# Attention keys split into a near band and far classes, and values projected by token: a change to a hybrid layer on one core

## The chip, the cores and the metric

The kernel runs on one core of a Trainium2 chip. The metric is the device time of one execution in microseconds (us), given as the median of several runs. Beside it stands one profiled execution, whose trace has the time of every instruction.

The engines are TensorE (PE in the profile, with its weight loads as PEld), VectorE (DVE), ScalarE (ACT), GpSimd (POOL) and SyncE (SP, which here only issues DMA transfers).

## The reference

One layer of a hybrid trunk, 1024 tokens of 1024 features, float32. The normalised input goes through one combined projection, whose columns feed two mixers: a gated delta rule (four heads of 128, chunked, with a short causal convolution) and a dilated attention (eight heads of 64). Their outputs are concatenated and projected, added to the input, and followed by a gated MLP. What the change touches is the attention:

```
DIL_PATTERNS = ((128, 1), (512, 4), (2048, 16))      # (window, dilation)
def dilated_attention(q, k, v):
    for window, dil in DIL_PATTERNS:                  # query t sees keys t, t-dil, ..., t-window
        num, den, m = band_attention(stride(qf), stride(kf), stride(vf), window // dil)
        ...
    out = sum(exp(m_i - m_all) * num_i) / sum(exp(m_i - m_all) * den_i)
```

Merging the branches by their denominators is the same as one softmax over all keys, in which a key that several branches see counts once per branch. A weight of 2 or 3 is a term log 2 or log 3 added to the score.

## The kernel before, in words

**Projections.** Every float32 matrix is split into a high and a low part in a faster format, and a product takes three matmuls (`mm3`: high x high, high x low, low x high). A projection tile is 128 columns of the combined weight: `raw_weight` loads 512 KB, `weight` splits them (high part on ScalarE, low part on VectorE), and 2 x 8 x 3 matmuls of 128 x 128 stationary weights and 512 moving tokens make 128 features x 1024 tokens. VectorE rescales the result by the token's norm. Raw tiles, high parts and low parts have two slots each, so a split waits until TensorE has left the tile two before. The loop is `dense` (line 477), its order is the list `DENSE` (line 42): one key tile of the delta rule, two attention tiles, four times queries and values of the delta rule, then the other ten attention tiles (of each of four head pairs: queries, keys, values), then four gate tiles (`z`). The attention's tiles are parked in DRAM (`apark`), with the tokens of each block of 128 sorted by class (token modulo 4), 32 tokens a class.

**Attention.** `attention` (line 865) works on four pairs of heads, eight blocks of 128 queries each, two blocks to a step. `att_load` reads queries, keys and values of a pair; `att_values` (line 844) transposes the values on TensorE to tokens x features (`vn`) and makes a second copy sorted by class (`vc`) with 16 small transfers. For each block, `scores` (line 884) makes the scores of the block itself and the one before it (the near part, 256 columns), and then the scores of each class of queries against the keys of the same class of blocks 0 to 3 (128 columns, for blocks 0 to 3) or 0 to 7 (256 columns, for blocks 4 to 7), near and even future ones among them; a mask with the multiplicities removes what is too much. The class products are 32 queries wide and several run side by side in the array. `softmax` (mask and minimum on VectorE, exponential on ScalarE, division on VectorE), `turn` (transposes, line 932), `values` (near part, line 946) and `merge_classes` (class part, line 955, once per four blocks) follow.

**Order.** A class `Weave` plays the streams (delta rule, attention, projections, output projection) against its own estimate of each engine's time and so fixes the order on TensorE by hand: every matmul gets a token. A stream with a lower number goes first when its operands are estimated ready; `dense` has the lowest rank and fills the gaps. So projection matmuls stand between the attention's steps. On the other engines and on SP's queue a scheduler orders the instructions at build time, and each engine then executes in that order; SP issues one DMA after the other, and one that waits for a semaphore holds those behind it. The recurrence (`chain`) starts when all its queries and values are projected and the blocks' inverses are merged (`forward_sub` on VectorE, `merge` on TensorE); `kprep` transposes the keys, makes their Gram products and stores blocks of them to DRAM; attention follows the chain; then the output projection and the MLP, which the change leaves as they are.

In the profile most instructions carry line 189 (`mm`), 193 (`tp`), 139 or 141 (the helper that records an engine's operation), so tiles are told apart by name: `sm` softmax, `pt` and `pb` its transposes (near and class part), `vn` and `vc` the values, `whi`, `wlo`, `xhi`, `xlo` the high and low parts of weights and input, `um` key blocks, `og` and `zz` the gate work, `olo` the output projection's split.

Of the kernel before, what the change touches and what calls it, by code (L numbers as in the profile page):

```python
# [7 lines left out]
F32 = mybir.dt.float32  # L8
# [7 lines left out]
P = 128  # L16
S = 1024
# [24 lines left out]
DENSE = ([("k", 3), ("a", 0, 0), ("a", 0, 1)] + [(c, h) for h in range(4) for c in "qv"] + [("a", 0, 2)]  # L42
         + [("a", p, i) for p in (1, 2, 3) for i in range(3)] + [("z", h) for h in range(4)])
# [101 lines left out]
def hybrid_layer(tc, I, out):  # L145
# [91 lines left out]
    apark = dp.tile([4, 3, P, S], F32, name="apark")  # L237
# [239 lines left out]
    def dense():  # L477
# [5 lines left out]
        raw = [raw_weight(I["wi"][0])]  # L483
        nxt = wk(None, raw.pop())
        raw.append(raw_weight(I["wi"][1]))
        for i, col in enumerate(DENSE):
            kind, h = col[:2]
            if kind == "z":
                yield from wv.until(("o", h))
            w = nxt  # L490
            if i + 1 < len(DENSE):
                nxt = wk(None, raw.pop())
            if i + 2 < len(DENSE):
                raw.append(raw_weight(I["wi"][i + 2]))
# [343 lines left out]
    def att_load(pi):  # L838
        qT, kT, vT = [A(nm, "uy") for nm in ("qT", "kT", "vT")]
        for i, t in ((2, vT), (0, qT), (1, kT)):  # L840
            sy.dma_start(t, apark[pi, i])
        return qT, kT, vT

    def att_values(vT):

        vn, vc = A("vn", "kt"), A("vc", "kt")
        for hh in range(2):
            pt = yield from next_bank("atr", vT, slack=ASLACK * (hh == 0))
            for c in range(4):
                i = 4 * hh + c  # L850
                tp(pt[:, c * P:(c + 1) * P], vT[:, i * P:(i + 1) * P])
            ac.activation(vn[:, half(hh)], pt, AF.Copy)
        queue = wv.free["sync"]
        for c in range(4):
            for n in range(4):
                sy.dma_start(vc[32 * n:32 * n + 32].rearrange("u (c b d) -> u c b d", c=4, b=2)[:, c],
                             vn[32 * c:32 * c + 32].rearrange("u (b n d) -> u n b d", b=2, n=4)[:, n])

        wv.ready[vc.tensor.name] = max(wv.pe, wv.ready[vn.tensor.name]) + 6.0
        wv.free["sync"] = max(wv.pe, queue) + 1.6  # L860
        return vn, vc
# [3 lines left out]
    def attention():  # L865
        for h in range(2):
            yield from wv.until(("c", h, NCH - 1))
        mks = [A("mk", "go") for _ in range(2)]
        sy.dma_start(mks[0], I["mk"][0])
        sy.dma_start(mks[1], I["mk"][1])  # L870
# [674 lines left out]
```

## Time and profile before

| what | us |
|---|---|
| median of three runs | 1243.48 |
| lowest and highest | 1238.09, 1244.25 |
| span of the profiled execution, first to last instruction | 1237.8 |
| TensorE busy in it | 1216.1 |
| VectorE busy | 960.1 |
| ScalarE busy | 576.7 |

The page of the profile gives no other time of the profiled execution beside its span, which is 0.3 us below the lowest run. In the trace the projections with the delta rule's preparation take roughly the first 200 us, the chain runs until about 290, the attention until about 500, and the output projection and the MLP take the rest.

### The profile page before, as it was taken

The page shows a single profiled execution, that of the slowest core. Times are in us where ns is not written, and L with a number is a line of the kernel's source. Part 1 is how long each engine was busy: PE and PEld are TensorE (multiplying, and loading weights), DVE is VectorE, ACT ScalarE, POOL GpSimd, SP SyncE. Part 2 cuts the span into 40 slices and gives each one's busy share as a digit, 9 for nine tenths or more (in the row PEclk, how much of TensorE's full clock was granted, in tenths as well). Part 3 has the DMA queues.
Part 4 walks back from the last instruction along what each step waited for, and adds up shares of the span by engine and source line. Part 5 has one row for each costly group of instructions (what it writes and reads, how often), then busy time and mean ns, then how long its engine had stood idle before and what let it go on. Part 6 is the DMA issues. An engine that isn't in the chain of part 4 may idle for free.

```text
span 1237.8 us, 18310 instructions
## 1 busy us (share of the span) xinstructions
PE 1216.1 (98%) x7040; PEld 1003.8 (81%) x7040; DVE 960.1 (78%) x1526; ACT 576.7 (47%) x1111; POOL 48.8 (4%) x34
## 2 busy tenths in 40 slices
PE   9999999999999999999999999999999999999996
PEld 7888887898777877788788888888888888788886
DVE  7686984573666758577889898898898989899875
ACT  7383344363443435455454454444444554344441
POOL 0211110022000000000000000000000000000000
PEclk9999999999999999999999999999999999999999
DMA  7423235245342311343321322312313298545623
GB/s 230 103 75 97 85 116 170 92 137 206 126 146 61 107 57 45 124 173 120 119 100 53 102 81 73 102 55 99 100 54 102 80 357 286 169 149 192 196 85 137
DMA packets 81975, 153.53 MB, mean 124 GB/s; under 512 B 21824, under 2 KB 32736, under 8 KB 81888
## 3 DMA queue, kind: packets, MB, share of 16 engines
q1 hardware_dynamic: 81888, 152.37, 37.7%
q8 instruction: 55, 0.90, 0.3%
q14 instruction: 32, 0.26, 0.1%
HBM read 114.31 MB, written 35.93 MB: 121 GB/s over the span
## 4 chain that ended last, share of the span: by engine, by line
PE 87%; DVE 7%; DMA 2%; issue 2%; ACT 1%; POOL 1%; POOLq 0%; DVEq 0%; ACTq 0%
PE ps L189 45%; PE pa L189 19%; PE dw L189 10%; PE pc L189 9%; PE ps L193 4%; DVE pr L139 2%; DMA wd<-in_wd 2%; DVE x1h L139 1%; DVE wd L139 1%; PE warm L189 1%; DMA wst<-in_wu 0%; DVE wlo L139 0%; DVE sm L141 0%; DVE t L139 0%; POOL rs L139 0%
## 5 line engine op out<-in xcount | busy, mean ns | idle before, releaser
L189 PE MATMUL dw<-pr 128*128 128x512 f32 (+1 forms) x984 | 212.5, 377 | 1.5 <-DVE x1h L139 1.3
L189 PEld LDWEIGHTS dw<-pr 128*128 128x128 f32 x984 | 176.2, 188 | 36.7 <-DVE x1h L139 3.3
L189 PE MATMUL ps<-xhi,whi 128*128 128x512 f32 x448 | 187.4, 418 | 0.0
L189 PE MATMUL ps<-xhi,wlo 128*128 128x512 f32 x448 | 176.2, 393 | 0.0
L189 PE MATMUL ps<-xlo,whi 128*128 128x512 f32 x448 | 175.4, 392 | 0.0
L189 PE MATMUL pa<-T,pair 128*128 128x512 f32 x528 | 127.1, 389 | 0.6 <-ACT u L139 0.6
L189 PEld LDWEIGHTS pa<-T,pair 128*128 128x128 f32 x528 | 98.9, 188 | 21.2 <-ACT u L139 0.7
L189 PEld LDWEIGHTS ps<-xhi,wlo 128*128 128x128 f32 x448 | 84.3, 188 | 18.8
L189 PEld LDWEIGHTS ps<-xhi,whi 128*128 128x128 f32 x448 | 84.7, 189 | 17.0 <-issue 3.3
L189 PEld LDWEIGHTS ps<-xlo,whi 128*128 128x128 f32 x448 | 84.9, 189 | 13.3
L139 ACT ACTIVATE u<-pa 128x512 f32<-128x512 f32 x44 | 26.3, 598 | 110.7 <-PE pa L189 110.7
L139 DVE SCALAR_TENSOR_TENSOR y<-xu,fcw,y 128x1023 f32<-128x1023 f32 (+1 forms) x44 | 56.3, 1280 | 25.7 <-ACT y L139 25.6
L139 ACT ACTIVATE whi<-wst 128x1024 fp32r<-128x1024 f32 (+2 forms) x38 | 38.5, 1013 | 58.2 <-PE ps L189 52.3
L189 PE MATMUL pc<-B,pair 128*128 128x512 f32 x264 | 63.4, 389 | 0.0
L189 PE MATMUL pa<-B,A 128*128 128x512 f32 x264 | 63.4, 389 | 0.0
L189 PE MATMUL pc<-T,S 128*128 128x512 f32 x264 | 63.4, 389 | 0.0
L189 PE MATMUL pa<-T,S 128*128 128x512 f32 x264 | 63.4, 389 | 0.0
L141 ACT ACTIVATE sm<-sm,mx 128x512 f32<-128x512 f32 (+2 forms) x64 | 41.2, 646 | 45.6 <-DVE mx L141 45.6
L139 DVE TENSOR_TENSOR wst<-wst 128x512 f32<-128x512 f32 x88 | 60.3, 686 | 0.8
L189 PE MATMUL ps<-B,pair 128*128 128x512 f32 x252 | 60.5, 389 | 0.0
L139 ACT ACTIVATE pr<-wd 128x1024 fp32r<-128x1024 f32 x33 | 34.9, 1058 | 49.6 <-DVE wd L139 28.3
L189 PEld LDWEIGHTS pc<-T,S 128*128 128x128 f32 x264 | 49.5, 188 | 10.3
(232 smaller groups left out, 2292.0 us busy)
## 6 DMA issues: line engine op xcount, KB each, us to landing
wst<-in_wu SPq DMA_DIRECT2D x44, 512.0 KB, 3.7
wd<-in_wd SPq DMA_DIRECT2D x44, 512.0 KB, 3.8
wst<-in_wi SPq DMA_DIRECT2D x25, 512.0 KB, 3.7
upark<-y SPq DMA_DIRECT2D x22, 512.0 KB, 3.7
apark<-aqkv SPq DMA_DIRECT2D x12, 512.0 KB, 2.8
r<-upark SPq DMA_DIRECT2D x11, 512.0 KB, 7.3
r<-upark SPq DMA_DIRECT2D x22, 256.0 KB, 7.2
wa<-in_wd SPq DMA_DIRECT2D x22, 256.0 KB, 2.7
```

What stands on the lines that cost most here:

```text
L139: return getattr(eng, op)(*a, **kw)
L141: return getattr(eng, op)(*a, **kw)
L189: tc.stamp_issue_order_token(nc.tensor.matmul(dst, lhs, rhs, start=start, stop=stop, **kw).ins, TOKEN)
L193: tc.stamp_issue_order_token(nc.tensor.transpose(dst, src, ident).ins, TOKEN)
```

## The change

It has three parts.

1. **Keys.** A block's class scores now cover only the blocks before its near part: blocks 0 and 1 have none, 2 and 3 have 64 columns, 4 and 5 have 128, 6 and 7 have 192. They stand ahead of the near scores in the row. The near mask now holds the multiplicities of all three branches, and one mask of 896 columns serves all blocks as a plain slice, where it was a strided view of two masks. `turn` transposes fewer 128-column pieces, and `merge_classes` uses 64 of the 128 class keys of the last group and only the blocks of queries that have it.
2. **Values.** The attention's value columns leave the list of tiles. They are projected to tokens x features straight away: the input's parts are stationary (128 tokens), the weights move (512 columns, all heads). Two groups of four token blocks, each with four weight tiles of 512 KB in which two of eight row blocks lie; the second group loads and splits the same weights again. ScalarE evicts with the token's norm as scale, and the result goes to DRAM (`vpark`). `att_values`, its transposes and its 16 transfers per pair go; `att_load` reads `vn` in four and `vc` in two transfers from `vpark`.
3. **Order.** In `DENSE` the two value groups stand right behind the first key tile, ahead of the delta rule's queries and values, where two attention tiles stood; eight attention tiles follow behind those.

```diff
-DENSE = ([("k", 3), ("a", 0, 0), ("a", 0, 1)] + [(c, h) for h in range(4) for c in "qv"] + [("a", 0, 2)]
-         + [("a", p, i) for p in (1, 2, 3) for i in range(3)] + [("z", h) for h in range(4)])
+DENSE = ([("k", 3), ("V", 0), ("V", 1)] + [(c, h) for h in range(4) for c in "qv"]
+         + [("a", p, i) for p in range(4) for i in range(2)] + [("z", h) for h in range(4)])
...
+        def values_by_token(g):
+            banks = [bank(t) for t in ("asc", "asc", "ch", "ch")]
+            for j in range(4):
+                w = [t.rearrange("p (k m) -> p k m", k=2) for t in take()]
+                for kk in range(2):
+                    k = 2 * j + kk
+                    for i, pt in enumerate(banks):
+                        c = 4 * g + i
+                        yield wv.need(pt, *w)
+                        mm3(pt, [t[:, c * P:(c + 1) * P] for t in xs[k]], [t[:, kk, :] for t in w], k == 0, k == KT - 1)
+            for i in range(0, 4, 2):
+                vx = A("vx", "ev", shape=(P, 2, 512))
+                for e in range(2):
+                    c = 4 * g + i + e
+                    ac.activation(vx[:, e, :], banks[i + e], AF.Copy, scale=rst[:, c:c + 1])
+                c = 4 * g + i
+                sy.dma_start(vpark[c * P:(c + 2) * P].rearrange("(e p) d -> p e d", e=2), vx)
+            wv.done.add(("V", g))
...
     def att_load(pi):
-        qT, kT, vT = [A(nm, "uy") for nm in ("qT", "kT", "vT")]
-        for i, t in ((2, vT), (0, qT), (1, kT)):
+        qT, kT = [A(nm, "uy") for nm in ("qT", "kT")]
+        for i, t in enumerate((qT, kT)):
             sy.dma_start(t, apark[pi, i])
...
+        for c in range(4):
+            sy.dma_start(v8(vn)[32 * c:32 * c + 32], by_class[c][:, :, cols])
...
+        for b in range(2):
+            sy.dma_start(vc.rearrange("p (b c d) -> p b c d", b=2, c=4)[:, b], rows[b][:, :, cols])
...
-                it["n1"] = (it["n"] + 1) * P - it["k0"]
-                it["wd"] = it["n1"] + P * it["nb"]
+                it["near"] = (n + 1) * P - it["k0"]
+                it["far"] = 64 * (n // 2)
+                it["wd"] = it["far"] + it["near"]
...
-                for c in range(4):
+                for c in range(4 if far else 0):
                     o = slice(32 * c, 32 * c + 32)
                     for e, er in enumerate(HALVES):
-                        mm(it["ps"][e][o, n1_:wd].rearrange("p (n u) -> p n u", u=32),
+                        mm(it["ps"][e][o, :far].rearrange("p (n u) -> p n u", u=32),
...
-                    for i in range(wd // P):
-                        tp(pp[:, i * P:(i + 1) * P], sm[:, e, i * P:(i + 1) * P])
-                    turned(it, e, pt, pp)
+                    for i in range(near // P):
+                        tp(pp[:, i * P:(i + 1) * P], sm[:, e, far + i * P:far + (i + 1) * P])
+                    for i in range(nf):
+                        tp(pp[:, near + i * P:near + (i + 1) * P], sm[:, e, i * P:(i + 1) * P])
...
+            parts = (((0, 128, 0), (1, 64, 2)) if hh else ((0, 64, 2),))
             for c in range(4):
-                for b in range(nb):
-                    for e in range(2):
+                for b, rows, u in parts:
+                    for e, er in enumerate(HALVES):
...
-                           vcv[:, c, b, er], g["pb"][e][:, :, b, 32 * c:32 * c + 32], 0.14,
+                           vcv[:rows, b, c, er], g["pb"][e][:rows, u:, b, 32 * c:32 * c + 32], 0.11 - 0.028 * u,
```

The number of matmuls that the projections take is the same before and after (25 tiles of 48, against 21 tiles of 48 and two groups of 96).

More of the change, by code (lines that the diff above doesn't have):

```diff
@@ L934, in turn @@
             for b, (it, tag) in enumerate(zip(pair, ("asc", "atr"))):
-                sm, wd, n1_ = it["sm"], it["wd"], it["n1"]
+                sm, near, far = it["sm"], it["near"], it["far"]
+                nf = -(-far // P)
                 it["pt"] = []
@@ L949, in values @@
                 u = it["u"]
-                for i in range(it["n1"] // P):
+                for i in range(it["near"] // P):
                     for e, er in enumerate(HALVES):
@@ L980, in attention, with advance @@
         pipe = []
-        def advance(pair, more=None):
+        def advance(pair):
             done = pipe.pop() if pipe else None
@@ L985, in advance @@
                 yield from turn(done)
-            if more is not None:
-                last["values"] = yield from more
             if pair is not None:
```

147 lines of the change are left out of this document (70 added, 77 removed).

## The prediction

> **What bounds the kernel now.** I read the busy shares first, then the chain that ended last, then windows by stage, because a share over the whole span hides where the slack is.
>
> ```profile
> PE 1216.1 (98%) x7040; PEld 1003.8 (81%) x7040; DVE 960.1 (78%) x1526; ACT 576.7 (47%) x1111; POOL 48.8 (4%) x34
> PE 87%; DVE 7%; DMA 2%; issue 2%; ACT 1%; POOL 1%; POOLq 0%; DVEq 0%; ACTq 0%
> 60.00:80.00 20.00, 20.00 (x101) 16.68 (x100) 18.16 (x25) 18.63 (x70) 1.64 (x1) 1.00 0.17 55
> 100.00:200.00 100.00, 100.00 (x572) 84.48 (x571) 80.63 (x162) 40.69 (x113) 15.14 (x9) 1.00 0.37 111
> 290.00:440.00 150.00, 150.00 (x1333) 118.70 (x1332) 93.95 (x244) 62.60 (x163) 4.48 (x2) 1.00 0.36 117
> 440.00:500.00 60.00, 55.26 (x506) 43.50 (x505) 43.80 (x101) 27.16 (x64) 0.00 (x0) 0.97 0.21 59
> ```
>
> The columns of a window are its length, then busy time of PE, PEld, DVE, ACT and POOL, the granted clock, DMA share and GB/s. TensorE is the bound and also the chain. In the attention stage (290 to 440) it is busy for 150.00 of 150.00 us, since projection products stand between the attention's steps as filler. So work taken from TensorE here comes off the end one for one, and work taken from VectorE, ScalarE or the queues counts only where TensorE waits: the last 60 us (4.74 us idle). From 60 to 80 us ScalarE has only 1.37 us to spare and VectorE 1.84; the change puts work just there.
>
> **The change on TensorE.** The counts are from the order of both built kernels' instructions; matmuls of plain f32 have two records each in the trace.
>
> ```profile
> L193 PE MATMUL ps<-ident,sm 128*128 128x128 f32 x216 | 29.3, 276 | 3.7 <-DVE sm L141 3.7
> L189 PE MATMUL ps<-pb,vc 128*64 128x128 f32 x192 | 12.0, 273 | 0.0
> L189 PEld LDWEIGHTS ps<-pb,vc 128*64 128x64 f32 x192 | 11.0, 137 | 0.0
> L189 PE MATMUL ps<-kT,qT 64*32 64x256 f32 x256 | 8.8, 382 | 0.0
> L189 PE MATMUL ps<-kT,qT 64*32 64x128 f32 x256 | 5.3, 275 | 0.0
> L189 PEld LDWEIGHTS ps<-kT,qT 64*32 64x32 f32 x512 | 7.1, 106 | 6.3 <-issue 5.3
> 62.07 1.04 PE L193 MATMUL ps<-ident,kT 128*128 128x128 f32 x8
> 62.86 0.47 PE L189 MATMUL ps<-xhi,whi 128*128 128x512 f32 x1
> 70.22 0.39 PE L189 MATMUL ps<-xhi,wlo 128*128 128x512 f32 x1
> 77.56 1.05 PE L189 MATMUL ps<-kT 128*128 128x128 f32 x8
> 78.37 0.48 PE L189 MATMUL ps<-xhi,whi 128*128 128x512 f32 x1
> ```
>
> Busy over count is the price here; the mean beside it holds the pipeline's latency.
>
> 1. Class scores. Now 256 records of 256 columns at 34.4 ns (8.8/256) and 256 of 128 at 20.7 ns (5.3/256): 14.1 us. After: none for blocks 0 and 1, and 128 records each of 64, 128 and 192 columns. On the straight line through both prices, 64 and 192 columns cost 13.9 and 27.5 ns; 13.9 is also what a weight load of this shape takes (7.1/512). That makes 128 x (13.9 + 20.7 + 27.5) = 7.9 us: **-6.2**. If 64 columns cost as much as 128, -5.3; if half of it, -6.7.
> 2. Transposes of the softmax: 216 to 184. Eight transposes take 0.79 us from start to start of what follows (62.07 to 62.86), 0.099 each: 32 fewer are **-3.2**; by the group's 0.136 (waits in it), -4.3.
> 3. Transposes of the values: 32 fewer of the same kind, **-3.2** (up to -4.3). Their eight evictions and 64 small transfers go too, at no gain: TensorE doesn't wait for them.
> 4. Class values. 192 records stay 192, but 128 of them have 64 columns instead of 128. By columns that would be 128 x 31 ns = 4.0 us. But a record takes 62.5 ns (12.0/192) and its weight load 57 ns (11.0/192), and the load has the same 64 columns of values as before: 128 x 5 ns, **-0.7**. The Trainium skill, "TensorE: Matmul & The Clock Gate", section "LDWEIGHTS (loading the stationary operand)", says that a load takes its columns over 1.2 in ns whatever its rows; an estimate by it is 53 ns, so at most -1.2, and the halved contraction (64 of 128 rows) buys nothing. The trace's 57 ns agrees, which is why I don't book the 4.0.
> 5. Values by token: 192 matmuls of 512 columns replace 192, the stationary and the moving operand swapped. 33 of them lie between 62.86 and 70.22, 32 steps of 0.23 us. Stationary tiles of 128 x 128 and moving ones of 512 columns are what every projection has: **0**, between -0.5 and +0.5.
>
> Sum on TensorE: **-13.3** (-10 to -18).
>
> **The wait that it may add.** A value group has four weight tiles of 24 products (24 x 0.23 = 5.5 us) where a projection tile has 48 (11.0 us), and each tile is split on ScalarE (high part) and then on VectorE (low part), in the slot that the tile two before leaves. Here the split, the transfer and the keys' preparation collide.
>
> ```profile
> 64.33 1.05 ACT L139 ACTIVATE whi<-wst 128x1024 fp32r<-128x1024 f32 x1
> 65.41 1.22 DVE L139 TENSOR_TENSOR wlo<-wst,whi 128x1024 fp32r<-128x1024 f32 x1 [0.46 <-ACT whi L139]
> 72.86 0.61 ACT L141 ACTIVATE ktok<-ps 128x512 f32<-128x512 f32 x1
> 75.29 1.10 ACT L139 ACTIVATE whi<-wst 128x1024 fp32r<-128x1024 f32 x1
> SPq L139 <- DVE um L139: 13.7, 3, 7.8
> wst<-in_wi SPq DMA_DIRECT2D x25, 512.0 KB, 3.7
> ```
>
> The new group starts where the first attention tile starts now, six products before 62.07, at 60.7. Tile 1 ends at 60.7 + 5.5 + 0.79 = 67.0. Tile 2 takes ScalarE's split at 64.33 (ScalarE's order up to there is unchanged), its low part is done at 65.41 + 1.22 = 66.6: in time. It ends at 67.0 + 5.5 + 0.79 (eight transposes) = 73.3. Tile 3's split stands on ScalarE where the key copy of 72.86 stands now: 73.9, low part 75.2 with a hand-over. Its second product needs that at 73.5: a wait of **+1.7 us**. Tile 4: between 72.86 and 75.29 ScalarE now does a copy, four squares and an activation, 2.4 us; another copy and two squares, about 1.0, also stand ahead of this split in the new order, so it starts at 73.9 + 3.4 = 77.3 and its low part is done at 79.6, while TensorE is at tile 3 until 75.2 + 23 x 0.23 + two groups of Gram products of 0.81 (77.56 to 78.37) = 82.1. No wait; the tiles behind it, whose splits need only 2.3 us of 5.5, come ahead likewise. On SP's queue, weight transfers now stand behind four groups of key-block stores and four value stores, which wait for VectorE and ScalarE; each is due some 10 us after its slot is free, the transfer takes 3.7, so a blocked queue (7.8 us at the longest now) could make one late. Bounds: 0, and three late tiles, 3 x 2.3 = +7.
>
> **The end of the attention.** The order moves here.
>
> ```profile
> 449.03 1.92 PE L189 MATMUL ps<-pb,vc 128*64 128x128 f32 x32
> 453.23 0.92 PE L193 MATMUL ps<-ident,sm 128*128 128x128 f32 x4 [2.28 <-DVE sm L141]
> 453.80 0.78 PE L189 MATMUL ps<-xhi,whi 128*128 128x512 f32 x1
> 456.08 0.63 PE L189 MATMUL ps<-xhi,wlo 128*128 128x512 f32 x1
> 452.00:455.00 3.00, 1.77 (x7) 1.55 (x8) 3.00 (x9) 1.02 (x4) 0.00 (x0) 0.75 0.03 11
> 455.00:458.00 3.00, 3.00 (x14) 2.42 (x13) 1.10 (x4) 0.28 (x1) 0.00 (x0) 0.68 0.23 87
> 479.46 1.06 PE L193 MATMUL ps<-ident,sm 128*128 128x128 f32 x8 [1.38 <-DVE sm L141]
> 487.58 1.09 PE L189 MATMUL ps<-pt,vn 128*64 128x128 f32 x16
> 488.06 0.68 DVE L141 CUSTOM_DVE_ANT_1 sm<-ps,mk 128x512 f32<-128x512 f32 x1
> 490.69 0.88 DVE L141 TENSOR_SCALAR sm<-sm,mx 128x512 f32<-128x512 f32 x2
> 492.84 1.91 PE L193 MATMUL ps<-ident,sm 128*128 128x128 f32 x16
> 499.47 0.50 PE L189 MATMUL ps<-ohi,whi 128*128 128x512 f32 x1
> ```
>
> The wait of 2.28 us comes from gate work on VectorE between the steps of a softmax. After it the granted clock reads 0.75 and 0.68 and the six products from 453.80 to 456.08 come 2.28/5 = 0.46 us apart instead of 0.23; six of them are 1.4 us, and with the transposes beside them I take 1.6. In the changed order that pair has widths 128 and 256 instead of 256 and 384, three products stand before its transposes, and the gate work stands before its first step: I take the wait and its slow stretch as gone, **-3.9**. Of the 1.38 I take half, **-0.7**. Against it, less filler is left at the very end, since the values went ahead: six products instead of 18 between the last scores and the last transposes. Now they are ready at 487.58 + 1.09 + 18 x 0.23 = 492.8, the first softmax at 490.69 + 0.88 = 491.6. After: TensorE is ready about 2.5 us after the scores; the softmax takes 3.5 us at 512 columns (488.06 to 491.6), some 3.1 at 448, and starts 0.4 after the scores: **+1.2** for both blocks. Net **-3.4**, between -6.4 (all 4.74 idle and 1.6 slow gone) and +4 (both waits stay, and the last one starts as late as its order allows).
>
> The Trainium skill, in the same page, section "What's actually happening", has the clock halved after an idle window of about 3.4 us. By it the 1.7 us above costs no clock, and neither should the 2.28 have; the trace shows that the 2.28 did and the 1.38 did not. So a stall somewhat over 2 us costs nearly double here, and the bounds count it so.
>
> **What costs nothing.** Narrower softmaxes (VectorE and ScalarE) and fewer rescaling evictions lie under TensorE's 150.00 of 150.00. The recurrence's forward substitution meets less work on VectorE (one head's queries and values less stand in it), and its results are wanted no sooner. Four more weight splits and the eight new evictions lie beside products, except for the wait above. The new loads of the values by token and by class wait on slots that the chain leaves, tens of products before the first scores; if one were late, the price is its landing, near the 3.7 us of a row above.
>
> **Sum.** -13.3 + 1.7 - 3.4 = **-15.0 us** on the profiled span of 1237.8, so 1222.8. The page gives no other time of that execution; the lowest run, 1238.09, is 0.3 above the span and the median, 1243.48, is 5.7 above. I set the change against the median: **1228.5**.
>
> **Rivals.**
> - *The splits become the path* (slower). If each split in the two value groups starts only when TensorE asks for it, each of eight tiles shows 1.05 + 1.22 = 2.3 us, and such gaps have cost 1.6 of clock: 8 x 3.9 = 31 in place of 1.7, so 1243.5 - 16.7 + 31 = about 1258. It decides where a split starts more than 5.5 - 2.3 = 3.2 us after its slot is free. For it: 18.63 of 20.00 on ScalarE, and the queue's waits. Against: the tiles after the fourth have room. Chance 0.10, with half-way cases (1243 to 1250) another 0.05.
> - *The filler is what runs out* (no change). With the values ahead, attention has 12 projection tiles to hide in instead of 14; if its chain sets the pace, the 13.3 turn into idle time: 1234 to 1243. Against: narrower steps shorten that chain too. Chance 0.20.
> - *The higher prices hold and no wait comes*: -18 at most on TensorE, with -4 to -6 at the end: about 1221, 1216 to 1224. Chance 0.15.
> - The forecast, 1224 to 1234: chance 0.50.
>
> That the change doesn't do what it says could be here only in the class values; booked above at -0.7.
>
> A measurement tells about 0.5% (6.2 us) from no change. Faster by more than that (below 1237.3): 0.50 + 0.15 + 0.08 of the second rival = 0.73; within it 0.17; slower 0.10. The range 1218 to 1243 leaves out about 0.05 below and 0.15 above.
>
> **What would show it.** Right: the windows from 290 on full as before, the stage's end (first output projection product, now at 499.5) about 15 us earlier, one wait for a low weight part near 73 us, no clock under 0.9 near the end. Wrong: several waits on weight parts from 60 to 115 us, waits on softmax tiles spread over the attention, or class-value records near 31 ns.

## The result and the profile after

The changed kernel takes 1233.59 us (median of four runs, 1232.33 to 1234.87). The kernel before took 1243.08 us in its four runs beside them. The ratio is 0.9929, with a 95% interval of 0.9906 to 0.9952: 9.5 us, 0.76%, faster. The forecast was 1228.5, and 15 us. So the sign and the range held, and a third of the gain is missing.

The profiled execution took 1232.33 us, with a span of 1230.2. The page's busy shares and its chain:

```profile
PE 1206.7 (98%) x6848; PEld 992.2 (81%) x6848; DVE 948.1 (77%) x1522; ACT 570.7 (46%) x1099; POOL 47.9 (4%) x34
PE 83%; DVE 9%; DMA 4%; issue 2%; ACT 2%; POOL 0%; SPq 0%; POOLq 0%; DVEq 0%; ACTq 0%
```

TensorE is still the bound. Its busy time fell by 9.4 us (from 1216.1), but its idle time rose by 1.8 (from 1237.8 - 1216.1 = 21.7 to 1230.2 - 1206.7 = 23.5). VectorE's share of the chain went from 7% to 9%: something now waits for it. The windows by stage, with the columns of the prediction, say where:

```profile
60.00:80.00 20.00, 19.19 (x98) 15.67 (x97) 17.19 (x24) 19.03 (x70) 1.64 (x1) 1.00 0.18 55
100.00:200.00 100.00, 100.00 (x653) 83.64 (x652) 71.46 (x143) 37.83 (x92) 10.38 (x7) 1.00 0.41 119
290.00:440.00 150.00, 147.75 (x1248) 116.94 (x1247) 93.39 (x267) 60.84 (x179) 12.63 (x8) 0.99 0.42 133
440.00:500.00 60.00, 56.69 (x483) 43.24 (x482) 46.39 (x107) 28.54 (x66) 0.00 (x0) 1.00 0.27 84
```

From 60 to 80 us TensorE now idles 0.8 us. From 290 to 440, where it had no idle moment, 2.25 us are idle and the clock is no longer full. In the last 60 us 3.3 us are idle, where it was 4.7. The groups of TensorE's instructions that the change touches (count, busy time, mean of one, idle time before):

```profile
L193 PE MATMUL ps<-ident,sm 128*128 128x128 f32 x184 | 26.5, 281 | 2.9 <-DVE sm L141 2.8
L189 PE MATMUL ps<-whi,xhi 128*128 128x512 f32 x64 | 26.3, 411 | 0.0
L189 PE MATMUL ps<-pb,vc 64*64 64x64 f32 x128 | 8.0, 233 | 0.0
L189 PE MATMUL ps<-pb,vc 128*64 128x128 f32 x64 | 7.0, 292 | 0.0
L193 PE MATMUL ps<-ident,vT 128*128 128x128 f32 x32 | 4.4, 276 | 0.0
L189 PE MATMUL ps<-kT,qT 64*32 64x192 f32 x128 | 3.5, 329 | 0.0
L189 PE MATMUL ps<-kT,qT 64*32 64x128 f32 x128 | 2.7, 275 | 0.0
L189 PE MATMUL ps<-kT,qT 64*32 64x64 f32 x128 | 1.8, 222 | 0.0
```

The class scores took 14.1 us and take 8.0. The class values (`pb,vc`) took 12.0 us and take 15.0, though two thirds of them have half the columns. Of these groups it is the one that went the wrong way.

TensorE's timeline near 340 us and at the attention's end (start, duration, what; in brackets the idle time before it and what ended it):

```profile
335.96 1.52 PE L189 MATMUL ps<-kT,qT 64*128 64x256 f32 x40
337.41 0.88 PE L189 MATMUL ps<-pt,vn 128*64 128x128 f32 x12
340.13 1.27 PE L193 MATMUL ps<-ident,sm 128*128 128x128 f32 x6 [1.84 <-DVE sm L141]
341.66 1.51 PE L193 MATMUL ps<-ident,sm 128*128 128x128 f32 x6 [0.26 <-DVE sm L141]
342.83 0.78 PE L189 MATMUL ps<-xhi,whi 128*128 128x512 f32 x1
...
478.00 1.51 PE L189 MATMUL ps<-kT,qT 64*128 64x256 f32 x34 [0.77 <-ACT pb L141]
...
483.97 1.06 PE L193 MATMUL ps<-ident,sm 128*128 128x128 f32 x8 [0.65 <-DVE sm L141]
...
487.17 0.87 PE L189 MATMUL ps<-pt,vn 128*64 128x128 f32 x7 [1.55 <-DVE pt L141]
...
490.46 0.50 PE L189 MATMUL ps<-ohi,whi 128*128 128x512 f32 x1
```

Between the scores at 335.96 and the transposes at 340.13 no projection product stands, and TensorE waits for the softmax. The output projection starts at 490.46, 9.0 us earlier than before (499.47).

**A mark to compare by.** The first matmul of the MLP ends the part that the change touches:

```profile
L189 PE MATMUL pa<-T,pair x528: 387/389/500, 601.1 to 1008.4; 128*128 128x512 f32 x176
```

That is the kernel before. The changed kernel:

```profile
L189 PE MATMUL pa<-T,pair x528: 388/389/481, 591.3 to 998.3; 128*128 128x512 f32 x176
```

It comes at 591.3 instead of 601.1, **9.8 us** earlier, close to the medians' 9.5. From the mark to the span's end it is 636.7 us before and 638.9 after. In all the profiles below this rest lies between 636.7 and 641.1, in no order that follows the edits, so I compare single profiles by the mark and whole kernels by their ratios.

### The profile page after: what moved, and what is told of

It reads as the page before. It is cut to its first block, busy times and chain, and to the rows that moved or that the text cites. A ratio compares the mean times of both kernels' runs of the same rounds, so it can differ in the third digit from the quotient of the medians.

```text
span 1230.2 us, 17841 instructions
## 1 busy us (share of the span) xinstructions
PE 1206.7 (98%) x6848; PEld 992.2 (81%) x6848; DVE 948.1 (77%) x1522; ACT 570.7 (46%) x1099; POOL 47.9 (4%) x34
## 4 chain that ended last, share of the span: by engine, by line
PE 83%; DVE 9%; DMA 4%; issue 2%; ACT 2%; POOL 0%; SPq 0%; POOLq 0%; DVEq 0%; ACTq 0%
PE ps L189 43%; PE pa L189 18%; PE pc L189 9%; PE dw L189 9%; PE ps L193 3%; DVE pr L139 2%; DMA wd<-in_wd 2%; DMA r<-upark 1%; DVE x1h L139 1%; DVE wd L139 1%; DVE kT L139 1%; DVE sm L141 1%; ACT dec L139 1%; PE warm L189 1%; DVE r L139 0%
## 5 line engine op out<-in xcount | busy, mean ns | idle before, releaser
L189 PE MATMUL ps<-xhi,whi 128*128 128x512 f32 x384 | 160.1, 417 | 0.0
L189 PE MATMUL ps<-xhi,wlo 128*128 128x512 f32 x384 | 150.5, 392 | 0.0
L189 PE MATMUL ps<-xlo,whi 128*128 128x512 f32 x384 | 150.1, 391 | 0.0
L189 PEld LDWEIGHTS ps<-xhi,wlo 128*128 128x128 f32 x384 | 72.2, 188 | 16.1 <-DVE wlo L139 0.3
L189 PEld LDWEIGHTS ps<-xhi,whi 128*128 128x128 f32 x384 | 72.4, 189 | 14.9 <-issue 2.6
L189 PEld LDWEIGHTS ps<-xlo,whi 128*128 128x128 f32 x384 | 72.6, 189 | 11.2
L139 ACT ACTIVATE whi<-wst 128x1024 fp32r<-128x1024 f32 (+2 forms) x42 | 42.9, 1022 | 69.7 <-PE ps L189 64.1
L141 ACT ACTIVATE sm<-sm,mx 128x320 f32<-128x320 f32 (+4 forms) x64 | 36.1, 565 | 63.1 <-DVE mx L141 63.1
L139 DVE TENSOR_TENSOR wlo<-wst,whi 128x1024 fp32r<-128x1024 f32 (+2 forms) x42 | 49.4, 1175 | 12.1 <-ACT whi L139 12.0
L189 PEld LDWEIGHTS pa<-B,A 128*128 128x128 f32 x264 | 49.6, 188 | 10.3
```

What stands on the lines that cost most here:

```text
L139: return getattr(eng, op)(*a, **kw)
L141: return getattr(eng, op)(*a, **kw)
L189: tc.stamp_issue_order_token(nc.tensor.matmul(dst, lhs, rhs, start=start, stop=stop, **kw).ins, TOKEN)
```

## The experiments

Theory: the missing third is the class values' price and TensorE's new waits in the attention, and these come from the place of the value groups. Rival: the parts cost what their records say, and the waits come from the narrower softmaxes. In the table "ahead" and "within" are projection products ahead of the attention's first scores and from there to its end, "output" those of the output projection that stand in it, all from the order of the built kernels' instructions; "first step" is the first softmax instruction in the trace. "Half clock" is the time between 60 us and the mark in which the granted clock read 0.5, from windows of one microsecond; work that falls into it takes twice its time, so it has cost at most half of its length.

| kernel | ahead | within | output | first step, us | mark, us | half clock, us | median, us | ratio to before, 95% |
|---|---|---|---|---|---|---|---|---|
| before | 927 | 417 | 0 | 313.0 | 601.1 | 3.4 | | |
| changed | 1002 | 342 | 0 | 329.3 | 591.3 | 3.4 | 1233.59 | 0.9929 (0.9906 to 0.9952) |
| e1 merge order | 1002 | 342 | 0 | 330.0 | 587.4 | 0 | 1230.08 | 0.9892 (0.9872 to 0.9911) |
| e2 values alone | 1002 | 342 | 24 | 331.4 | 605.2 | 3.4 | 1247.53 | 1.0032 (1.0019 to 1.0045) |
| e3 keys alone | 927 | 402 | 0 | 311.8 | 589.4 | 0 | 1231.49 | 0.9908 (0.9887 to 0.9928) |
| e4 filler before turn | 1002 | 342 | 42 | 330.0 | 603.0 | 13.7 | 1245.13 | 1.0019 (1.0006 to 1.0031) |
| e5 position alone | 1011 | 333 | 42 | 333.1 | 615.2 | 17.1 | 1254.13 | 1.0096 (1.0079 to 1.0114) |
| e6 keys, merge order | 927 | 402 | 0 | 312.2 | 585.7 | 0 | 1228.64 | 0.9897 (0.9878 to 0.9916) |
| e7 last evictions | 1002 | 342 | 0 | 329.6 | 587.8 | 3.4 | 1229.93 | 0.9902 (0.9885 to 0.9919) |
| e8 rows 128 | 1002 | 342 | 0 | 330.5 | 588.2 | 3.4 | 1228.20 | 0.9891 (0.9873 to 0.9908) |
| e9 values late | 900 | 414 | 0 | 314.5 | 588.8 | 6.8 | 1230.41 | 0.9907 (0.9888 to 0.9926) |
| e10 late, some filler | 900 | 429 | 0 | 315.4 | 589.6 | 3.4 | 1230.31 | 0.9903 (0.9884 to 0.9922) |
| e11 values mid | 1098 | 246 | 42 | 349.6 | 604.4 | 23.9 | 1245.98 | 1.0022 (1.0008 to 1.0037) |
| e12 plan, values ready | 1002 | 342 | 24 | 330.0 | 595.4 | 10.2 | 1236.01 | 0.9943 (0.9920 to 0.9967) |

### The price of the class values: e1, e8, e6

e1, the changed kernel with two lines exchanged:

```diff
-            for c in range(4):
-                for b, rows, u in parts:
+            for b, rows, u in parts:
+                for c in range(4):
```

> Same work as the changed kernel, only the order of the second half's 32 class-value matmuls differs: the 16 with 128 stationary rows first, then the 16 with 64 rows, instead of pairs in turn. Theory (the price lies in switching between stationary tiles of 64 and of 128 rows): the stretch of such a merge falls from 2.57 us (32 matmuls, 80 ns each) to about 16 x 58 + 16 x 39 = 1.55 us, and the four of them give back about 4 us: 0.9967 of the changed kernel's time. Rival (each record simply costs what it costs, 64 rows or 128, and the order is nothing): the stretch stays at 2.5 us and the time within 0.1 per cent.

The stretch of one merge of the second half in the changed kernel, to the start of what follows:

```profile
366.67 2.54 PE L189 MATMUL ps<-pb,vc 128*64 128x128 f32 x32
369.14 0.50 PE L189 MATMUL ps<-xhi,whi 128*128 128x512 f32 x1
```

and in e1:

```profile
366.21 1.65 PE L189 MATMUL ps<-pb,vc 128*64 128x128 f32 x32
367.79 0.50 PE L189 MATMUL ps<-xhi,whi 128*128 128x512 f32 x1
```

2.47 us became 1.58 in each of the four merges, 3.6 us in all, and the order alone did that. The mark came 3.9 us earlier. That holds two things more, which partly cancel: e1 reaches the scores near 336 us 0.68 us later (336.64 against 335.96), and the half clock behind the wait near 340 us is missing in it. e8 keeps the order and gives all tiles 128 rows. Its output then holds products of keys that do not belong to it, so it serves for the time of the merges only.

```diff
-            parts = (((0, 128, 0), (1, 64, 2)) if hh else ((0, 64, 2),))
+            parts = (((0, 128, 0), (1, 128, 2)) if hh else ((0, 128, 2),))
```

> The changed kernel, but the 64-row class-value matmuls take all 128 rows (so their output has products of keys that do not belong to it); the moving columns, 64, and the order are the changed kernel's. Theory (the price lies in switching the number of stationary rows): the second half's merge falls from 2.57 us to about 1.6 us although the order alternates, and the time by about 4 us; the first half's 16 matmuls stay near 0.62 us if the columns set their price and go to 1.0 us if the rows do. Rival (alternating widths of the moving operand, 128 and 64 columns, cost it): 2.57 us stays.

The same merge in e8:

```profile
367.69 1.51 PE L189 MATMUL ps<-pb,vc 128*64 128x128 f32 x32
369.13 0.50 PE L189 MATMUL ps<-xhi,whi 128*128 128x512 f32 x1
```

It takes 1.44 us, though 128 and 64 moving columns still alternate. So the rival (widths) falls: the price lies in switching the stationary tile between 128 and 64 rows. The weight loads show how. Their groups in the changed kernel (busy, mean, idle time before):

```profile
L189 PEld LDWEIGHTS ps<-pb,vc 64*64 64x64 f32 x128 | 5.3, 132 | 3.4 <-issue 3.4
L189 PEld LDWEIGHTS ps<-pb,vc 128*64 128x64 f32 x64 | 3.6, 135 | 0.8
```

and in e8:

```profile
L189 PEld LDWEIGHTS ps<-pb,vc 128*64 128x64 f32 x192 | 8.5, 137 | 0.0
```

With one number of rows the loads follow each other without a gap; with two, the loads stand still for 4.2 us in all, waiting for nothing that the profile shows (1.4 us in e1, where the rows change less often). The Trainium skill, "TensorE: Matmul & The Clock Gate", section "Step-by-step: what each phase is for", says that a weight load is pulled ahead of running matmuls when the row groups don't conflict or when it goes to a background buffer. That the pull ahead fails at a change of rows fits these gaps, but no run here shows the array's inside. The first half's 16 records (no switch of rows) took 0.97 us before, with 128 columns (333.00 to 333.97). With 64 columns they took 0.61 in the changed kernel (347.54 to 348.15) and 0.57 with 128 rows in e8 (348.63 to 349.20): the moving columns set their price, not the rows.

e6 is the same exchange in the kernel with the keys alone (e3, below).

> The narrower keys alone, with the second half's class values ordered by stationary rows (the 128-row block first). Theory (switching rows costs 1 us per merge, and the values' move is a loss): 4 us under the keys alone, about 1227.5, and the fastest so far. Rival (the saving of the order was filler-bound or drift): within 1 us of the keys alone, 1231.5.

The mark moved by 3.7 us (589.4 to 585.7) and the median by 2.9. The two ratios' intervals overlap, and they come from two sets of runs of the kernel before; the mark and the merges carry it.

### The parts by themselves: e2, e3, e5

e2 is the changed kernel with the scores, masks, transposes and class values of before; e3 is the kernel before with those of the changed kernel, and its values projected and transposed as before. Both exchange the functions from `scores` to `merge_classes` and the masks as a whole.

> Only the values projected by token, ahead of the queries; scores, masks and class values as in the kernel before. Theory: TensorE loses the 32 value transposes (-3.2 to -4.0 us) and waits some 1 us in the value groups; the mid-attention wait of 2 us does not come, since the softmaxes keep their width; so 3 us under the kernel before, give or take 1.5. Rival (moving the values ahead takes filler from the attention, and this is what ate the gain): waits on softmax tiles near 330 to 345 and near the attention's end come here too, and the time is within 1 us of the kernel before or above it.

> Only the narrower scores, masks and class values; the values are projected and transposed as in the kernel before. Theory (the narrow softmaxes let the order put transposes with nothing ahead of them): class scores -6.1, softmax transposes -3, class values +1.6, so -7.5 at most, and a wait of about 2 us with a slowed clock shows at a pair of 320 columns: -4 to -7.5 us against the kernel before. Rival (the waits come from the values' move): no such wait, the full -7.5.

The keys alone give at least as much as the whole change: the mark at -11.7 us against -9.8 (up to 1.7 of the difference is the changed kernel's half clock), and 0.9908 against 0.9929, with intervals that overlap. The values alone lose: +4.1 at the mark, 1.0032. For the values the rival was right and my theory wrong by 7 us; for the keys the rival was right that the wait near 340 us does not come, and the full -7.5 was too little, since the waits at the attention's end go as well (4.74 us of idle time from 440 to 500 became 0.89). The two largest waits in e2 from 430 to 530 us:

```profile
PE ps L193 <- DVE sm L141: 4.2, 2, 2.8
PE ps L189 <- ACT pb L141: 1.8, 3, 0.8
```

e5 separates the values' place from what they are: the kernel before, with four attention tiles instead of two ahead of the queries.

```diff
-DENSE = ([("k", 3), ("a", 0, 0), ("a", 0, 1)] + [(c, h) for h in range(4) for c in "qv"] + [("a", 0, 2)]
-         + [("a", p, i) for p in (1, 2, 3) for i in range(3)] + [("z", h) for h in range(4)])
+DENSE = ([("k", 3)] + [("a", p, i) for p in range(4) for i in range(3)][:4] + [(c, h) for h in range(4) for c in "qv"]
+         + [("a", p, i) for p in range(4) for i in range(3)][4:] + [("z", h) for h in range(4)])
```

> The kernel before with one edit: four attention tiles instead of two are projected ahead of the queries and values of the recurrence; nothing else. In the order of its instructions 1011 projection products then stand ahead of the first attention transposes and 333 within the attention, against 927 and 417 before (1002 and 342 in the changed kernel). Theory (what the value groups cost is their place: products spent early are missing as filler at the attention's end): waits of several us on softmax tiles between 450 and 520 us, and a time 5 to 9 us over the kernel before, that is, more than the values alone lost (4.4), since here no transposes are saved. Rival (the value groups themselves cost it, by their four banks, their splits and their evictions): the place alone is worth less than 2 us.

The time rose by 0.96%, 12 us, more than expected. Up to about half of that is the clock: behind its waits e5 runs at half clock for 17.1 us, the kernel before for 3.4. The two largest waits from 430 to 530 us in e5:

```profile
PE ps L189 <- ACT pb L141: 6.0, 3, 4.4
PE ps L193 <- DVE sm L141: 5.2, 2, 4.0
```

The first softmax steps, in the kernel before and in e5:

```profile
313.00 0.42 DVE L141 CUSTOM_DVE_ANT_1 sm<-ps,mk 128x256 f32<-128x256 f32 x1 [3.52 <-issue]
```

```profile
333.12 0.42 DVE L141 CUSTOM_DVE_ANT_1 sm<-ps,mk 128x256 f32<-128x256 f32 x1
```

This is the mechanism. What is projected ahead of the queries delays the recurrence, and the attention, which waits for the recurrence, begins 20 us later. TensorE is full in the meantime: it works off projection products. But their number is fixed, 1344 in all, and those spent early are missing as filler in the attention. The attention's own steps (score, softmax, transpose) keep their length, and at the end they show. The changed kernel spends 75 products more ahead. At 0.227 us each, the median spacing of two of them from 100 to 200 us, that is 17.0 us; its attention begins 16.3 us later. In e3, e6, e9 and e10 the table's two counts make less than 1344: there 15 to 30 products are left over behind the attention. In these four TensorE is busy for 59.1 us or more from 440 to 500 us, in all the others for 58.3 or less. This is e3:

```profile
440.00:500.00 60.00, 59.11 (x465) 45.54 (x464) 41.39 (x87) 23.89 (x53) 0.00 (x0) 1.00 0.26 82
```

The narrower keys need less filler, so with them the same loss of place seems to cost less: the mark says +1.9 from e3 to the changed kernel and +1.7 from e6 to e1, where without them it is +4.1. The first of these has up to 1.7 us of half clock in it, and the second does not show in the ratios (0.9897 and 0.9892).

Against e5, at nearly the same place, e2 is 10.0 us better at the mark; up to almost 7 of these are e5's longer time at half clock. So projecting by token is a gain in itself, of the transposes (4.0 by their group); whether the attention step that they made adds to it is not shown. The place takes the gain back.

### Is the filler really finite: e4, e12, e11

e4 and e12 leave the work and the number of products as they are and only change where the planner puts them. e4 is the changed kernel with

```diff
-TSLACK = -1.0, -0.6
+TSLACK = 0.0, 0.0
```

> The changed kernel with one number of its planner changed: transposes of a softmax are no longer issued up to 1.0 (0.6) us before the plan expects their input, but when it is expected. Theory (TensorE stood for 1.84 and 0.26 us and ran at a clock of 0.83 only because no projection product was put there): the wait near 340 us goes with its slow stretch, 3 to 4 us, and some of it returns at the attention's end, where the products spent are missing: 1 to 3 us under the changed kernel. Rival (the filler is what runs out): the same number of us turns up as waits between 470 and 490 us, time within 0.5 us or longer.

The rival was right, and far more than it said: the time is 1.0019 of before, 0.9% over the changed kernel. Its two largest waits from 430 us on:

```profile
PE ps L193 <- DVE sm L141: 4.8, 1, 4.8
PE ps L189 <- DVE pt L141: 3.4, 1, 3.4
```

The planner put three to six products more into most steps, ran out of them, drew 42 products of the output projection into the attention, and where none could go TensorE stood still. Behind these waits the clock was at half for 13.7 us, against 3.4 in the changed kernel.

For e12 I looked at why nothing stood ahead of the transposes near 340 us. The planner's own estimates have the answer: the product that first reads the values of a head pair (`vn`) waits 4.1 us in the plan, since the loads by token land late in its model, and during such a wait no projection product is placed. On the chip that product, at 337.41 above, did not wait. e12 is e1 with one line at the end of `att_load`:

```diff
+        wv.ready[vn.tensor.name] = wv.ready[vc.tensor.name] = wv.pe
```

> The first experiment's kernel (changed kernel, class values ordered by rows), and the planner no longer takes the values by token of a head pair to arrive late: in its plan the first product that reads them waited 4.1 us, in which it placed no projection product, while the trace shows no wait there. In the new order 15 and 3 products stand around the transposes near 340 us, where none stood. Theory A (the wait of 1.84 us near 340 us was this wrong estimate and nothing else): it goes, 2 us under the first experiment. Theory B (there are only 342 products for the attention; one spent here is missing at the end): the wait near 340 us goes, but the projections run out earlier, 24 products of the output projection and then waits of more than 5 us stand between the attention's last steps, and the time is 3 to 12 us over the first experiment.

Theory B. The wait near 340 us went, and the window from 290 to 440 is full again; the next is not:

```profile
290.00:440.00 150.00, 149.85 (x1275) 119.95 (x1273) 95.56 (x265) 60.37 (x174) 13.29 (x8) 1.00 0.44 137
440.00:500.00 60.00, 50.98 (x451) 39.07 (x448) 43.86 (x111) 29.39 (x72) 0.00 (x0) 0.91 0.25 75
```

2.4 us less idle time there bought 5.7 us more here and a slower clock. The ratio is 0.9943 against e1's 0.9892. So the wrong estimate that made a wait also saved products for the end, where they were worth more.

e11 is the changed kernel with the groups behind the first head's query and value:

```diff
-DENSE = ([("k", 3), ("V", 0), ("V", 1)] + [(c, h) for h in range(4) for c in "qv"]
-         + [("a", p, i) for p in range(4) for i in range(2)] + [("z", h) for h in range(4)])
+DENSE = ([("k", 3), ("a", 0, 0), ("a", 0, 1)] + [("q", 0), ("v", 0)] + [("V", 0), ("V", 1)] + [(c, h) for h in range(1, 4) for c in "qv"]
+         + [("a", p, i) for p in range(1, 4) for i in range(2)] + [("z", h) for h in range(4)])
```

> The changed kernel with the two value groups moved behind the first head's query and value, on their four banks as in the changed kernel; two attention tiles stand ahead of the queries again. 1098 products stand ahead of the attention's first transposes and 246 within it. Theory (what counts is how many products are left when the attention begins): 96 fewer than in the changed kernel, and so waits of 10 to 20 us between 440 and 530 us: 0.5 to 1.5 per cent over the changed kernel. Rival (the place ahead of the queries is what hurts, whatever is left): faster than the changed kernel, since the recurrence starts earlier.

0.93% over the changed kernel, as the theory had it. The waits on softmax and class tiles from 430 to 530 us are 8.3 us, less than it said; the clock, 0.89 from 440 to 500 us, takes up to another 0.11 x 60 = 6.6. The rival was not put to the test: the attention's first step came at 349.6 us, the latest of all.

### Can the values have a better place: e9, e10

e9 is e1 with the values behind the recurrence's queries and values, on the two banks of the other projections:

```diff
-DENSE = ([("k", 3), ("V", 0), ("V", 1)] + [(c, h) for h in range(4) for c in "qv"]
-         + [("a", p, i) for p in range(4) for i in range(2)] + [("z", h) for h in range(4)])
+DENSE = ([("k", 3), ("a", 0, 0), ("a", 0, 1)] + [(c, h) for h in range(4) for c in "qv"] + [("V", g) for g in range(4)]
+         + [("a", p, i) for p in range(1, 4) for i in range(2)] + [("z", h) for h in range(4)])
...
-            banks = [bank(t) for t in ("asc", "asc", "ch", "ch")]
+            banks = [bank("hf") for _ in range(2)]
...
```

> The changed kernel with the merge order of the first experiment, and the values by token moved behind the recurrence's queries and values, in four groups of two token blocks on the two banks of the other projections (each weight tile is loaded and split four times instead of twice); two attention tiles stand ahead of the queries again. 900 projection products stand ahead of the attention's first transposes and 414 within it (changed kernel 1002 and 342, before 927 and 417). Theory (the loss of the values is their place alone): the waits between 470 and 490 us (3.3 us) and those of the value groups near 72 us (1.0 to 1.8) go, so 3 to 5 us under the first experiment: about 0.986 of the kernel before. Rival (splits: a weight tile has only 12 products, 2.7 us, for a split of 2.3 us): waits for weight parts spread over 180 to 300 us, and a time at the first experiment's or above.

The waits between 470 and 490 us and near 72 us went, as the theory said. But the time is e1's. The idle time moved to the recurrence: from 200 to 290 us TensorE is busy for 84.5 us of 90, where it is 88.8 in the changed kernel, and e9 runs at half clock for 6.8 us from 270 to 305 us, where e1 does not. Of the waits for weight parts that the rival feared only two came, 1.1 and 0.8 us; the others are for tiles of the recurrence (`vtok` 2.2, `w` 1.6, `r` 1.1). Neither text had that.

e10 changes e9's `TSLACK` to -0.9, -0.5.

> The kernel of the ninth run with the planner's allowance for early transposes at -0.9 and -0.5 instead of -1.0 and -0.6, which puts products between the scores and the transposes at three of the four places where none stand (429 products within the attention). Theory (filler is enough now, so filling a wait is a gain): 2 to 4 us under the ninth run if such waits show there. Rival (the products are missing at the end, as in the fourth run): at or above the ninth run.

It is e9's time, 1230.31. The waits that it was to fill do not exist in e9 (no wait on a softmax tile among those listed), so this run tells nothing about filler.

### The last eviction: e7

e7 is e1 with

```diff
-                    uv.tensor_copy(pt[:, :near], pp[:, :near])
+                    if it["g"]["pi"] == 3 and it["n"] > 5:
+                        ua.activation(pt[:, :near], pp[:, :near], AF.Copy)
+                    else:
+                        uv.tensor_copy(pt[:, :near], pp[:, :near])
```

What stands ahead of that copy on VectorE in the changed kernel (the copy is the last row):

```profile
484.43 1.22 DVE L139 TENSOR_TENSOR wlo<-wst,whi 128x1024 fp32r<-128x1024 f32 x1
485.56 1.22 DVE L139 SCALAR_TENSOR_TENSOR zz<-zz,xr 128x1024 f32<-128x1024 f32 x1
486.70 0.75 DVE L141 COPY pt<-ps 128x256 f32<-128x256 f32 x2
```

> The changed kernel with the merge order of the first experiment, and the last two blocks' transposed near parts of the last head pair copied out of PSUM on ScalarE instead of VectorE. Theory (the wait of 1.55 us for the last near tile stands behind a weight split and a gate product on VectorE, 2.3 us): that wait goes, -1.5 us against the first experiment's 1230.1, if the splits of the attention's output are not later by as much. Rival (something behind it, the output's splits on ScalarE, comes as much later): within 0.5 us of 1230.1.

The wait of 1.55 us went: from 440 to 500 us TensorE is busy for 58.31 us, where it is 56.66 in e1. But the clock reads 0.97 there instead of 1.00, and the mark is e1's (587.8 and 587.4). The slow stretch sits here, in a window of e7:

```profile
475.00:480.00 5.00, 5.00 (x55) 3.75 (x55) 3.16 (x11) 2.72 (x8) 0.00 (x0) 0.66 0.26 97
```

0.34 x 5 = 1.7 us, what the wait gave. The waits just ahead of it, 0.24 and 0.77 us, stand in e1 too, at 473.46 and 474.93, and the clock stays full there. The rival was right in the number and wrong in the reason; whether the copy on ScalarE is worth something stays open.

The best versions here that compute the layer are e1 (0.9892) and e6 (0.9897), and they cannot be told apart. With the merge ordered, the values by token add nothing to the keys.

## Why the prediction was right, and where it was not

Forecast and measurement, step by step, in us:

| step | forecast | measured |
|---|---|---|
| class scores | -6.2 | -6.1 (14.1 to 8.0) |
| softmax transposes | -3.2 | -2.8 (29.3 to 26.5, part of it at a slow clock) |
| value transposes | -3.2 | -4.0 (8.4 to 4.4) |
| class values | -0.7 | +1.0 by stretches, +3.0 by the groups |
| values by token | 0 | -0.8 (192 x 0.397, where the projections took 0.401 each) |
| wait in the value groups | +1.7 | +1.0 (60 to 100 us) |
| wait and slow clock near 340 us | none | +3.8 |
| end of the attention | -3.4 | -3.0 (idle 4.7 to 3.3, and the slow stretch of 1.6) |
| sum at the mark | -15.0 | -9.8 |

The terms are read from groups and windows that overlap a little, so they need not add up to the last line.

1. **Class scores: right, to 0.1 us.** 64, 128 and 192 columns cost 14.1, 21.1 and 27.3 ns (1.8, 2.7 and 3.5 us over 128); the straight line through the two known prices gave 13.9, 20.7 and 27.5.
2. **Class values: the step that failed on TensorE, twice.** "The load has the same 64 columns of values as before: 128 x 5 ns" took the 57 ns of a weight load as a floor. It is none: 16 records of 64 columns follow each other in 0.61 us, 38 ns each with their loads, and e1's two groups of class values come to 9.8 us. The 57 ns goes with the 128 moving columns beside it: in e8, where two thirds of the loads stand beside 64, a load takes 44 ns (8.5/192). The rule of the Trainium skill that I weighed there ("TensorE: Matmul & The Clock Gate", section "LDWEIGHTS (loading the stationary operand)": columns over 1.2) gives an estimate of 53 ns for a load. The 38 ns lie under it, so it is no floor for the spacing; its other half, that rows don't matter, holds for a row of equal tiles (0.61 and 0.57 us). Before, a merge of 32 took 1.85 us (359.43 to 361.28) and one of 16 took 0.97; ordered by rows the term is 4 x (1.58 + 0.61 - 1.85 - 0.97) = -2.5 us. The switch of rows then adds 4 x 0.89 = 3.6 us in the order that the change has. I counted records and columns and did not look at what alternates with what.
3. **The value groups' wait: ScalarE was right, the wait was another.** ScalarE has no room from 60 to 80 us, as said, but no weight part is late, and the wait for one near 73 us is not there. Eight decay tiles (2.46 us; in the kernel before 2.47, at 69.82) stand on ScalarE ahead of the squares of the keys:

```profile
68.91 2.46 ACT L139 ACTIVATE dec<-dec,ngc 128x128 f32<-128x128 f32 x8
...
71.61 0.27 ACT L141 ACTIVATE sq<-ps 128x128 f32<-128x128 f32 x1
```

   and the next transposes on TensorE wait for the bank that the squares read:

```profile
72.03 0.66 PE L193 MATMUL ps<-ident,kT 128*128 128x128 f32 x4 [0.73 <-ACT sq L141]
```

   That the sum was near (1.0 us against 1.7) is luck.

4. **The end: the sum right, the parts not.** The wait of 2.28 us and its slow stretch went, as forecast. The little filler left brought +1.2 in the forecast; in the trace it is three waits that were not there (0.21, 0.77 and 0.65 us from 475 to 484) and one of 1.55 us for a near tile, where the kernel before has 0.26 and 0.82:

```profile
496.81 0.87 PE L189 MATMUL ps<-pt,vn 128*64 128x128 f32 x7 [0.82 <-DVE pt L141]
```

   The forecast left these last two out. That -3.4 and -3.0 agree is in part luck.

5. **"What costs nothing" failed for the loads by token.** "If one were late, the price is its landing." None was late. But the planner believed it, and so left the wait near 340 us: 1.84 + 0.26 us, and 1.7 more at a halved clock. I followed instructions and transfers, and not what the planner's estimates would make of them.
6. **The rival that I gave 0.20, "the filler is what runs out", is behind a part of what is missing.** I counted 12 tiles instead of 14 and let the narrower steps pay for that. They did not quite: the values' part, -3.2 + 1.7 + 1.2 = -0.3 in the forecast, is +1.9 by the mark between e3 and the changed kernel, and +4.1 alone. That is 2.2 of the 5.2 us that are missing at the mark, with up to 1.7 of half clock near 340 us in them; another 1.7 are the class values (point 2), and the rest I cannot tell apart. The forecast's own band (1224 to 1234) just holds the result, and the rival's (1234 to 1243) begins there.
7. The slower rival, splits as the path, did not come: no wait for a weight part longer than 0.8 us stands in the changed kernel.

## What to carry to other kernels

Where an off-path stage is hidden under filler, count the filler as a stock: a piece of it moved ahead is missing at the stage that later runs dry (in e5 19.1 us of products cost 14.1 at the mark; in e2, which saves transposes, 17.0 us cost 4.1), and whether a wait in the middle is worth filling depends on what those products are worth at the end. When a matmul shrinks, look at its neighbours in the order too: equal stationary shapes next to each other took 1.58 us where alternating ones took 2.47. And test the parts of a change by themselves; here one part alone was worth at least as much as the whole.

## What the hardware showed besides

**The length of a wait alone does not decide the clock after it.** The same wait of 1.84 us near 340 us stands in the changed kernel, e1, e7 and e8. The granted clock, in slices of a microsecond behind it, in the changed kernel:

```profile
341.00:342.00 1.00, 0.74 (x4) 0.37 (x3) 1.00 (x4) 0.28 (x1) 0.00 (x0) 0.50 0.00 0
342.00:343.00 1.00, 1.00 (x7) 1.00 (x6) 0.57 (x2) 0.28 (x1) 0.00 (x0) 0.50 0.00 0
```

and in e1:

```profile
341.50:342.50 1.00, 0.43 (x5) 0.31 (x4) 1.00 (x4) 0.28 (x1) 0.00 (x0) 1.00 0.00 0
342.50:343.50 1.00, 1.00 (x9) 0.92 (x8) 0.92 (x3) 0.54 (x2) 0.00 (x0) 1.00 0.00 0
```

In e8 it was halved as in the changed kernel, in e7 not. Between 60 us and the MLP, over all profiles, every single wait of 2.28 us or more led into a stretch at half clock. Below that it went both ways. Waits of 1.55, 2.21 (e10) and 2.24 us (e12) left the clock alone:

```profile
454.13 0.52 PE L193 MATMUL ps<-ident,sm 128*128 128x128 f32 x2 [2.24 <-DVE sm L141]
454.00:460.00 6.00, 5.87 (x29) 4.59 (x31) 1.97 (x9) 0.00 (x0) 0.00 (x0) 1.00 0.07 25
```

Waits of 1.06 (e3) and 1.12 us (e9) did not, and in e11 a stretch that began at 467 us had only waits of 0.81, 0.65 and 0.76 us just ahead of it. A stretch lasted 3.4 us, which cost up to 1.7 us, or two to four times as long (13.7 us in e11 from 467 us). The Trainium skill, "TensorE: Matmul & The Clock Gate", section "What's actually happening", has the activity window running freely, not started by the kernel. By it, up to 1.7 us of the changed kernel's profile hang on where that window stood. These rows agree with it, but no run here moves a wait against the window by itself. A single profile cannot settle an edit of that size (e7).
